# Three weight sums moved from GpSimd to VectorE, and a new written order around the second RMS norm, in a one-core encoder block

## The chip, the cores and the metric

The kernel runs on one core of one Trainium2 chip. The metric is device time in microseconds; the kernel before takes 1011.7 us, the median of three runs (1011.38 to 1012.49). A core has five engines with a queue of instructions each, worked off in order: TensorE (PE in the profile) multiplies matrices into PSUM, VectorE (DVE) does elementwise work, ScalarE (ACT) functions and casts, GpSimd (POOL) elementwise work from SBUF, and SyncE (SP) issues most of the transfers. Semaphores order the engines against each other.

## What is computed

One layer of a hybrid encoder block for 1024 tokens of width 1024, cut here to what matters:

```python
h = rms_norm(x, norm1_g);  q, k, v, u = split(h @ w_in)
a = neighbourhood_attention(rms_norm(q), rms_norm(k), v, rpb)      # 8 heads x 64, window 8 x 16
p = multiscale_pool(u, w_pool, pool_scale)                         # windows 2, 4, 8, 16
x = x + concat(a, p) @ w_out
h2 = rms_norm(x, norm2_g)                                          # x * rsqrt(mean(x*x) + 1e-6) * g
x = x + (silu(h2 @ w_gate) * (h2 @ w_up)) @ w_down                 # D_FF = 2816
```

All of it is in float32.

## The kernel before, in words

**Number format.** TensorE's products are made from split operands. `split(h, l, src)` (L114) casts `src` to a high part `h` on ScalarE (L115) and subtracts it on VectorE for the low part `l` (L116); a product then takes three matmuls, high x high, high x low and low x high. So each operand of each product costs one ScalarE cast and one VectorE subtraction before TensorE can read it.

**Stages.** The projections, the attention and the pooling come first, then the output projection `w_out` (L802), whose tiles `pw` are added into `x2` by VectorE (L818), then the gate and up projections in 22 chunks, and then the down projection. Activations lie transposed, with channels on the partitions. The tokens stand in two halves, `hf` 0 and 1, and the channels in eight blocks, two to an `x2` tile, so `x2[0..3]` is the first token half and `x2[4..7]` the second.

**Gate and up.** A chunk `i` is one pair of column blocks of the gate or the up weights; the chunks alternate between gate and up. A chunk is multiplied as a 2 x 2 block matrix with seven block products in place of eight, in the manner of Strassen and Winograd. `first`, `second`, `part_y`, `part_z`, `part_w`, `part_4` and `part_5` (L1079 to L1132) are these seven, twelve matmuls each. They need sums of weight blocks and of activation blocks:

- `fetch_w(i)` (L1008) loads the raw weights of a chunk in two transfers, issued by SyncE when buffers come free.
- `sum_w(i)` (L1022) makes the three sums s1, s2 and s3, three instructions of 128 x 512 (L1028 to L1030). By default they run on GpSimd; for chunk 3 the call names VectorE.
- `sum_4(i)` (L1018) makes the fourth sum on GpSimd (L1020).
- `cook_w(i, o)` (L1033) splits the weight operand `o`.
- `split_op(o, q, src)` (L999) splits an activation operand, 128 x 1024 per instruction.

**The second norm.** For each half, the squares of `x2` are made on ScalarE (`square`, L948; `square1`, L963), added up (on GpSimd, L950 and `fold`, L956, or on VectorE, L1204), split by `tok_split` (L929) and summed over the partitions by TensorE against a matrix of ones: `tok_sum` (L934), two matmuls, tile `ss`. `scale2(hf)` (L968) makes one over the root: v = mean + eps on VectorE (L973), Ln and Exp on ScalarE (L977, L978), and one correction step of Newton's on VectorE (L979 to L981). `norm2(hf, q)` (L983) multiplies `x2` by the gain and the result (two instructions, L989). For the second half, three `tok_sum` calls stand between `first(0)` and `first(1)` on TensorE's queue, for the tiles `a1`, `s6` and `s7`.

**The order.** From L1154 to L1319 the order on TensorE, ScalarE, VectorE and GpSimd is the order of the text (`pin`, `pin_act`, `pin_dve`, `pin_pool`). Behind that, from chunk 4 on (L1321), the scheduler of the framework puts the instructions of each engine in order, with times of its own. `park` (L1134) makes four sums of the results on GpSimd and stores them. Temporary tiles come from a pool of 45 buffers (`slot`); a load waits until its buffer is free.

Of the kernel before, what the change touches and what calls it, by code (L numbers as in the profile page):

```python
# [9 lines left out]
F32 = mybir.dt.float32  # L10
F32R = mybir.dt.float32r
AF = mybir.ActivationFunctionType
ALU = mybir.AluOpType
# [3 lines left out]
P = 128  # L17
DM = 1024
# [7 lines left out]
EPS = 1e-6  # L26
# [23 lines left out]
def hybrid_block(ctx, tc, xT, xt, w1, wu, rpbx, wpool, wout, wgu, wd, sm, out):  # L50
    nc = tc.nc
# [11 lines left out]
    def slot(dt, name, shape=None):  # L63
        return sp.tile(shape or [P, 1024], dt, tag="t4", name=name)
# [37 lines left out]
    def keep(i):  # L102
        if pin_act:
            tc.keep_in_program_order(i)

    def keepd(i):
        if pin_dve:
            tc.keep_in_program_order(i)

    def keepp(i):  # L110
        if pin_pool:
            tc.keep_in_program_order(i)

    def split(h, l, src):  # L114
        keep(nc.scalar.copy(h, src))  # L115
        keepd(nc.vector.tensor_tensor(out=l, in0=src, in1=h.bitcast(F32), op=ALU.subtract))  # L116
# [32 lines left out]
    def cook_w1_(p, kk):  # L149
        hs = slot(F32R, f"w1h_{p}_{kk}", [P, 2, 384])  # L150
        ls = slot(F32R, f"w1l_{p}_{kk}", [P, 2, 384])
        for i in range(2):
            wp_h[p, 2 * kk + i] = hs[:, i, :]
            wp_l[p, 2 * kk + i] = ls[:, i, :]
        if p == kk == 0:
            raw = raws.pop(("w1", 0, 0))
            keepd(nc.vector.tensor_copy(hs[:, 0], raw[:, 0]))
            yield
            keepd(
                nc.vector.tensor_tensor(out=ls[:, 0], in0=raw[:, 0], in1=hs[:, 0].bitcast(F32), op=ALU.subtract)  # L160
            )
            yield
            split(hs[:, 1], ls[:, 1], raw[:, 1])
        else:
            cook(("w1", p, kk), hs, ls)
# [322 lines left out]
    for i in range(4):  # L488
# [3 lines left out]
        else:  # L492
            g = cook_w1_(0, 0)
# [23 lines left out]
    for t in (6, 7):  # L517
        for k in range(KE, KC):
# [12 lines left out]
            out=qscale, in0=gqk[:, 0:1], scalar=-(HD**-0.5), in1=gqk[:, 1:2], op0=ALU.mult, op1=ALU.mult  # L531
# [270 lines left out]
    def w_out(t, nh, cs, n):  # L802
        ps = bank(stp if n else mmp, f"pw_{t}_{nh}_{n}")
        os_ = slice(t % 4 * P, t % 4 * P + P)
        o, hf = 4 * nh + t % 4, t // 4
        for i, c in enumerate(cs):
            mm3(
                ps,
                wo[c, nh, 0][:, os_],
                wo[c, nh, 1][:, os_],  # L810
                mix[c, hf, 0],
                mix[c, hf, 1],
                i == 0,
                i == len(cs) - 1,
            )
            yield
        x = x2[o // 2 + 4 * hf][:, o % 2]
        keepd(nc.vector.tensor_tensor(out=x, in0=ps, in1=x, op=ALU.add))  # L818
# [8 lines left out]
    x2 = []  # L827
# [89 lines left out]
    op_ = ctx.enter_context(tc.tile_pool(name="op", bufs=1))  # L917
    ones = op_.tile([P, P], F32R, name="ones2")
    nc.gpsimd.memset(ones.bitcast(F32), 1.0)
    ACTO = {}  # L920

    def act_op(o):
        ACTO[o] = [
            [slot(F32R, f"b{o}_{q}_{nm}", [P, 2, 512]) for nm in "hl"] for q in range(2)
        ]

    n2, ps2 = {}, {}

    def tok_split(src, nm):  # L929
        hl = slot(F32R, f"sq_hl_{nm}", [P, 2, 512])  # L930
        split(hl[:, 0], hl[:, 1], src)
        return hl
# [8 lines left out]
    def store(hf, q):  # L941
        keep(nc.scalar.dma_start(out=x2d[q + 4 * hf], in_=x2[q + 4 * hf]))
# [3 lines left out]
    def square(hf, q):  # L946
        s = slot(F32, f"sq_{hf}_{q}", [P, 2, 512])
        keep(nc.scalar.activation(s, x2[q + 4 * hf], AF.Square))  # L948
        if q:
            keepp(nc.gpsimd.tensor_tensor(out=acc[hf], in0=acc[hf], in1=s, op=ALU.add))  # L950
        else:
            acc[hf] = s

    def fold(hf):
        a = acc[hf]
        keepp(nc.gpsimd.tensor_tensor(out=a[:, 0], in0=a[:, 0], in1=a[:, 1], op=ALU.add))  # L956

    def square1(k):
        x = x2[4 + k // 2][:, k % 2]
        if k % 2 == 0:  # L960
            sq1.append(slot(F32, f"sq_1_{k}", [P, 2, 512]))
        r = sq1[-1][:, k % 2]
        keep(nc.scalar.activation(r, x, AF.Square))  # L963
        return r

    sq1 = []

    def scale2(hf):  # L968
        n = slot(F32, f"n2_{hf}", [P, 2, 512])
        n2[hf] = y = slot(F32, f"y2_{hf}", [P, 512])  # L970
        v, a = n[:, 0], n[:, 1]
        keepd(
            nc.vector.tensor_scalar(  # L973
                out=v, in0=ps2[hf], scalar1=1.0 / DM, scalar2=EPS, op0=ALU.mult, op1=ALU.add
            )
        )
        keep(nc.scalar.activation(a, v, AF.Ln))  # L977
        keep(nc.scalar.activation(y, a, AF.Exp, scale=-0.5))  # L978
        keepd(nc.vector.tensor_tensor(out=a, in0=y, in1=y, op=ALU.mult))  # L979
        keepd(nc.vector.scalar_tensor_tensor(out=a, in0=a, scalar=-0.5, in1=v, op0=ALU.mult, op1=ALU.mult))  # L980
        keepd(nc.vector.scalar_tensor_tensor(out=y, in0=a, scalar=1.5, in1=y, op0=ALU.add, op1=ALU.mult))  # L981

    def norm2(hf, *qs):  # L983
        for q in qs:
            x = x2[q + 4 * hf]
            for i in range(2):
                k = 2 * q + i
                keepd(
                    nc.vector.scalar_tensor_tensor(  # L989
                        out=x[:, i],  # L990
                        in0=x[:, i],
                        scalar=g2_sb[:, k : k + 1],
                        in1=n2[hf],
                        op0=ALU.mult,
                        op1=ALU.mult,
                    )
                )

    def split_op(o, q, src):  # L999
        split(*ACTO[o][q], src)  # L1000

# [16 lines left out]
    def sum_4(i):  # L1018
        x = sums[i]["12"]
        keepp(nc.gpsimd.tensor_tensor(out=x, in0=x, in1=sums[i]["s2"], op=ALU.subtract))  # L1020

    def sum_w(i, eng=nc.gpsimd, keep_=keepp):  # L1022
        m, f = MF[i]
        r0, r1 = raww[i]
        sa = slot(F32, f"sa_{m}_{f}", [P, 2, 512])
        s1, s2 = sa[:, 0], sa[:, 1]
        tt = eng.tensor_tensor
        keep_(tt(out=s1, in0=r0[:, 1], in1=r1[:, 1], op=ALU.add))  # L1028
        keep_(tt(out=s2, in0=s1, in1=r0[:, 0], op=ALU.subtract))
        keep_(tt(out=r0[:, 1], in0=r0[:, 0], in1=r0[:, 1], op=ALU.subtract))  # L1030
        sums[i]["s1"], sums[i]["s2"] = s1, s2

    def cook_w(i, o):  # L1033
        if i < EARLY and o in ("11", "12"):
            w = rg.tile([P, 2, 512], F32R, tag="w", name=f"w_{i}_{o}")
        else:
            w = slot(F32R, f"w_{i}_{o}", [P, 2, 512])
        wop[i, o] = w
        if o == "s4" and i > EARLY:
            sum_4(i)  # L1040
        split(w[:, 0], w[:, 1], sums[i][o])

    def product(i, ps, wo_, bo, chain, parts=range(4)):
        w = wop.pop((i, wo_))
        for k in range(4):
            h, l = ACTO[bo][k // 2]
            sl = slice(k * P, k * P + P)
# [102 lines left out]
    def w_full(t, nh, cs=eight, n=2):  # L1150
        for _ in w_out(t, nh, cs, n):
            pass
# [16 lines left out]
    store(1, 0)  # L1169
    fold(0)  # L1170
    hl = tok_split(acc[0][:, 0], "a0")
    for i in range(2):
        for o in ("11", "12"):
            cook_w(i, o)
    for o in ("11", "21"):
        act_op(o)
    w_full(6, 0)
    for i in range(2):
        sum_w(i)
    g = w_out(7, 0, eight, 2)  # L1180
    for _ in range(5):
        next(g)
    tok_sum(0, hl, True, True)
    scale2(0)
    for _ in g:
        pass
    square(1, 1)
    store(1, 1)
    fold(1)
    norm2(0, 0)  # L1190
    split_op("11", 0, x2[0])
    norm2(0, 1)
    fetch_w(2)
    w_full(4, 1)
    r4 = square1(4)
    split_op("11", 1, x2[1])
    sum_w(2)
    norm2(0, 2)
    split_op("21", 0, x2[2])
    w_full(5, 1)  # L1200
    a1 = acc[1][:, 0]
    r5 = square1(5)
    for r in (r4, r5):
        keepd(nc.vector.tensor_tensor(out=a1, in0=a1, in1=r, op=ALU.add))  # L1204
    hl = [tok_split(a1, "a1")]
    norm2(0, 3)
    split_op("21", 1, x2[3])
    store(1, 2)
    for i in range(2):
        sum_4(i)  # L1210
    cook_w(2, "11")
    w_full(6, 1)
    hl.append(tok_split(square1(6), "s6"))
    cook_w(2, "12")
    sum_4(2)
    w_full(7, 1)
    hl.append(tok_split(square1(7), "s7"))
    store(1, 3)
    xs = [bank(stp, f"x_{i}") for i in range(EARLY)]
    first(0, xs[0])  # L1220
    for i in range(3):
        tok_sum(1, hl[i], i == 0, i == 2)
    scale2(1)
    first(1, xs[1])
    fetch_w(3)
# [22 lines left out]
    cook_w(2, "s2")  # L1248
    settle(2, 0, 0, xs[2])
    sum_w(3, nc.vector, keepd)  # L1250
    sum_4(3)
    cook_w(3, "s2")
    act_op("t3")
# [216 lines left out]
    for n in range(len(works)):  # L1470
        g, k = divmod(n, 7)
        last = g == len(DGROUPS) - 1
        o, bo = ORDER[k]
# [99 lines left out]
```

## Time and profile before

| what | value |
|---|---|
| median of three runs | 1011.7 us |
| the profiled execution | 1012.01 us |
| its span in the profile | 1010.0 us |
| TensorE busy | 991.3 us (98%) |
| VectorE busy | 685.1 us (68%) |
| ScalarE busy | 415.7 us (41%) |
| GpSimd busy | 390.6 us (39%) |
| granted TensorE clock, mean | 0.993 |

The profile is one execution. Times in the timeline are microseconds from the start of the span. A row of the timeline reads: start, duration, engine, line, instruction, output tile <- input tiles, shapes, count, and in brackets how long the engine was idle before and which engine and line ended that wait. Neighbouring equal instructions are merged into one row with their count. A row of the waits reads: engine, tile and line <- what it waited for: total us, times, longest. A row of the windows gives, for each engine, the busy time in a stretch, then the granted share of TensorE's clock and the share of the DMA engines that was busy. "PEld" is TensorE's loading of weights, which overlaps its products.

The engines start a VectorE or ScalarE instruction a little before the one ahead has ended, so the distance from start to start is the cost in a full queue, not the duration.

### The profile page before, as it was taken

To read this page: it belongs to the slowest core of one execution; us is meant where nothing else is said; L and a number is where in the kernel's file an instruction comes from. 1 tells how busy PE (TensorE), PEld (TensorE's weight loads), DVE (VectorE), ACT (ScalarE), POOL (GpSimd) and SP (SyncE) were. 2 spreads that over 40 slices of the span, in tenths; PEclk is the share of its full clock that TensorE was granted. 3 is DMA by queue.
4 is the path that set the end of the run, shared out by engine and by line. 5 is a ranking of instruction groups with operands and counts; after the bars stand their busy time and mean duration, and the time that the engine had idled before them with its cause. 6 is when DMAs were issued, how large, how long until landed. Compare 5 with 4: busy or idle time off the path is not lost.

```text
span 1010.0 us, 13253 instructions
## 1 busy us (share of the span) xinstructions
PE 991.3 (98%) x4801; PEld 843.0 (83%) x4801; DVE 685.1 (68%) x1078; ACT 415.7 (41%) x797; POOL 390.6 (39%) x423
## 2 busy tenths in 40 slices
PE   9999999999999959999999999999999999999998
PEld 9988999998888848888888888888888888888887
DVE  5778777657843769877975555555462599888872
ACT  6634666656643234443333233233242254432500
POOL 0001434333422730059867846746733400000170
PEclk9999999999999979999999999999999999999999
DMA  9412742347813220123433322322317983373302
GB/s 352 185 58 88 221 127 73 96 140 249 267 55 139 95 83 1 41 85 115 155 116 116 132 77 104 126 83 105 120 51 243 355 291 127 104 242 113 125 32 94
DMA packets 56177, 135.88 MB, mean 135 GB/s; under 512 B 5872, under 2 KB 14832, under 8 KB 56112
## 3 DMA queue, kind: packets, MB, share of 16 engines
q1 hardware_dynamic: 48032, 106.45, 31.7%
q0 software_dynamic: 6784, 24.38, 6.4%
q10 hardware_dynamic: 1296, 4.21, 1.0%
q8 instruction: 38, 0.62, 0.3%
q14 instruction: 27, 0.22, 0.1%
HBM read 98.05 MB, written 32.77 MB: 130 GB/s over the span
## 4 chain that ended last, share of the span: by engine, by line
PE 85%; DVE 5%; POOL 5%; ACT 2%; issue 2%; DMA 1%; POOLq 0%; ACTq 0%; DVEq 0%
PE pj L85 12%; PE x L85 10%; PE z L85 10%; PE w L85 10%; PE pc L85 6%; PE pa L85 6%; PE pd L85 6%; PE pw L85 5%; PE y L85 5%; PE pu L85 4%; PE pb L85 3%; PE po L85 3%; PE s L85 2%; PE pt L90 2%; POOL gr L1138 1%
## 5 line engine op out<-in xcount | busy, mean ns | idle before, releaser
L85 PE MATMUL x<-b_h,w 128*128 128x512 f32 x352 | 116.3, 394 | 0.0
L85 PE MATMUL pw<-mx,wo 128*128 128x512 f32 x384 | 90.7, 392 | 0.4 <-DVE kl L116 0.4
L85 PE MATMUL pj<-w1h,xh 128*128 128x384 f32 x256 | 87.4, 346 | 1.6 <-DVE vnl L302 1.6
L622 POOL TENSOR_SCALAR e<-e,r 64x128 f32<-64x128 f32 (+2 forms) x96 | 53.8, 576 | 83.0 <-DVE r L617 42.2
L85 PE MATMUL pj<-w1l,xh 128*128 128x384 f32 x256 | 84.8, 335 | 1.0 <-DVE w1l L116 1.0
L85 PEld LDWEIGHTS pw<-mx,wo 128*128 128x128 f32 x384 | 71.0, 188 | 15.4 <-DVE kl L116 0.8
L85 PE MATMUL pj<-w1h,xl 128*128 128x384 f32 x256 | 83.8, 335 | 0.0
L1498 POOL TENSOR_TENSOR x2r<-x2r,u 128x512 f32<-128x512 f32 x12 | 23.8, 2020 | 149.8 <-ACT dbt_h L115 149.8
L1077 POOL TENSOR_TENSOR ur<-ur,gr 128x512 f32<-128x512 f32 x33 | 52.6, 1596 | 74.1 <-DVE ur L1068 31.8
L85 PEld LDWEIGHTS x<-b_h,w 128*128 128x128 f32 x352 | 67.1, 191 | 14.1
L85 PE MATMUL x<-b_l,w 128*128 128x512 f32 x176 | 69.2, 393 | 0.0
L116 DVE TENSOR_TENSOR w_s<-sa,w_s 128x512 fp32r<-128x512 f32 x44 | 52.6, 1196 | 21.9 <-ACT w_s L115 21.7
L115 ACT CAST a_h<-raw_a 128x1024 fp32r<-128x1024 f32 (+1 forms) x42 | 41.0, 978 | 49.3 <-PE pc L85 13.8
L85 PE MATMUL z<-bt_h,w 128*128 128x512 f32 x176 | 57.9, 390 | 0.5 <-DVE gr L1068 0.5
L85 PE MATMUL w<-b_h,w_s 128*128 128x512 f32 x176 | 57.9, 390 | 0.0
L85 PE MATMUL z<-bt_h,w_s 128*128 128x512 f32 x176 | 57.8, 389 | 0.0
L85 PE MATMUL w<-bt_h,w_s 128*128 128x512 f32 x176 | 57.8, 389 | 0.0
L85 PE MATMUL y<-bt_h,w_s 128*128 128x512 f32 x176 | 57.3, 389 | 0.0
L116 DVE TENSOR_TENSOR a_l<-raw_a,a_h 128x1024 fp32r<-128x1024 f32 (+1 forms) x42 | 49.7, 1188 | 3.4 <-ACT a_h L115 3.1
L85 PEld LDWEIGHTS pj<-w1h,xh 128*128 128x128 f32 x256 | 48.5, 190 | 2.8 <-DVE vnl L302 2.3
L85 PEld LDWEIGHTS pj<-w1l,xh 128*128 128x128 f32 x256 | 48.1, 188 | 1.4 <-DVE w1l L116 1.4
L85 PEld LDWEIGHTS pj<-w1h,xl 128*128 128x128 f32 x256 | 48.0, 188 | 0.0
(268 smaller groups left out, 2654.2 us busy)
## 6 DMA issues: line engine op xcount, KB each, us to landing
raw_a<-gsd SPq DMA_DIRECT2D x77, 256.0 KB, 3.7
raw_g<-in_wgu SPq DMA_DIRECT2D x22, 512.0 KB, 4.2
raw_u<-in_wgu SPq DMA_DIRECT2D x22, 512.0 KB, 3.9
gsd<-gr POOLq DMA_DIRECT2D x22, 512.0 KB, 4.0
raw_d<-in_wd SPq DMA_DIRECT2D x20, 512.0 KB, 4.6
nb<-in_rpbx SPq DMA_DIRECT2D x24, 384.0 KB, 4.1
raw_w<-in_w SPq DMA_DIRECT2D x15, 384.0 KB, 4.2
gsd<-ur POOLq DMA_DIRECT2D x11, 512.0 KB, 3.3
```

The costliest lines, as they stand in the source:

```text
L85: i = nc.tensor.matmul(*a, **k)
L90: i = nc.tensor.transpose(*a)
L115: keep(nc.scalar.copy(h, src))
L116: keepd(nc.vector.tensor_tensor(out=l, in0=src, in1=h.bitcast(F32), op=ALU.subtract))
L622: nc.gpsimd.tensor_scalar(out=out, in0=in0, scalar1=s1, scalar2=1.0, op0=ALU.mult, op1=ALU.mult)
L1077: k(eng.tensor_tensor(out=res[i][c][:, l], in0=src, in1=g, op=ALU.mult))
L1138: tt = lambda **k: keepp(nc.gpsimd.tensor_tensor(**k))
L1498: nc.gpsimd.tensor_tensor(out=q, in0=q, in1=U2[c], op=ALU.add)
```

## The change

- `sum_w(0)`, `sum_w(1)` and `sum_w(2)` are issued on VectorE (they were on GpSimd), at other places of the order.
- `scale2`: Ln reads the sum in PSUM itself, with scale 1/1024 and a bias tile `eps`; the square of the Exp result is made on ScalarE and no longer by L979 on VectorE; `scale2` takes a list of functions that it issues between the square and the rest of the correction step. v is still made on VectorE.
- For the first half that list holds `seven`: the rest of output tile `(7, 0)`, its square, store and fold, `sum_w(1)` and `sum_4(1)`. `sum_4(0)` is put ahead of `scale2(0)`.
- The splits of the first operands (`"11"`, `"21"`), the `norm2` calls and the splits for the token sums are put in another order, in which a `norm2` or another VectorE instruction stands between a cast and its low part.
- `fetch_w(2)` and `w_full(4, 1)` stand one `norm2` earlier; `cook_w(1, ...)` stands behind `w_full(6, 0)`; `sum_4(2)` stands behind `sum_w(3)`.

```diff
+    eps = op_.tile([P, 1], F32, name="eps")
+    nc.gpsimd.memset(eps, EPS)
...
-    def scale2(hf):
+    def scale2(hf, between=()):
...
-        keep(nc.scalar.activation(a, v, AF.Ln))
+        keep(nc.scalar.activation(a, ps2[hf], AF.Ln, scale=1.0 / DM, bias=eps))
         keep(nc.scalar.activation(y, a, AF.Exp, scale=-0.5))
-        keepd(nc.vector.tensor_tensor(out=a, in0=y, in1=y, op=ALU.mult))
+        keep(nc.scalar.activation(a, y, AF.Square))
+        for f in between:
+            f()
         keepd(nc.vector.scalar_tensor_tensor(out=a, in0=a, scalar=-0.5, in1=v, op0=ALU.mult, op1=ALU.mult))
...
     hl = tok_split(acc[0][:, 0], "a0")
-    for i in range(2):
-        for o in ("11", "12"):
-            cook_w(i, o)
     for o in ("11", "21"):
         act_op(o)
+    cook_w(0, "11")
+    cook_w(0, "12")
     w_full(6, 0)
-    for i in range(2):
-        sum_w(i)
+    cook_w(1, "11")
+    cook_w(1, "12")
+    sum_w(0, nc.vector, keepd)
     g = w_out(7, 0, eight, 2)
     for _ in range(5):
         next(g)
     tok_sum(0, hl, True, True)
-    scale2(0)
-    for _ in g:
-        pass
-    square(1, 1)
-    store(1, 1)
-    fold(1)
+
+    def seven():
+        for _ in g:
+            pass
+        square(1, 1)
+        store(1, 1)
+        fold(1)
+        sum_w(1, nc.vector, keepd)
+        sum_4(1)
+
+    sum_4(0)
+    scale2(0, (seven,))
     norm2(0, 0)
-    split_op("11", 0, x2[0])
-    norm2(0, 1)
     fetch_w(2)
     w_full(4, 1)
     r4 = square1(4)
+    norm2(0, 1)
+    split_op("11", 0, x2[0])
+    norm2(0, 2)
     split_op("11", 1, x2[1])
-    sum_w(2)
-    norm2(0, 2)
-    split_op("21", 0, x2[2])
     w_full(5, 1)
     a1 = acc[1][:, 0]
     r5 = square1(5)
+    norm2(0, 3)
     for r in (r4, r5):
         keepd(nc.vector.tensor_tensor(out=a1, in0=a1, in1=r, op=ALU.add))
+    split_op("21", 0, x2[2])
     hl = [tok_split(a1, "a1")]
-    norm2(0, 3)
     split_op("21", 1, x2[3])
     store(1, 2)
-    for i in range(2):
-        sum_4(i)
+    w_full(6, 1)
+    r6 = square1(6)
+    sum_w(2, nc.vector, keepd)
+    hl.append(tok_split(r6, "s6"))
+    w_full(7, 1)
+    r7 = square1(7)
     cook_w(2, "11")
-    w_full(6, 1)
-    hl.append(tok_split(square1(6), "s6"))
+    hl.append(tok_split(r7, "s7"))
     cook_w(2, "12")
-    sum_4(2)
-    w_full(7, 1)
-    hl.append(tok_split(square1(7), "s7"))
     store(1, 3)
...
     sum_w(3, nc.vector, keepd)
+    sum_4(2)
     sum_4(3)
```

## The prediction

> **What bounds the kernel now.** I read the page first, then TensorE's waits, then the stretch that holds them in windows and engine by engine in the timeline. The page gives the span; the profiled run itself took 1012.01 us, 2.0 us more than its span, and lies 0.3 us above the median of 1011.7.
>
> ```profile
> span 1010.0 us, 13253 instructions
> ```
>
> TensorE's waits (total, times, longest):
>
> ```profile
> PE ss L85 <- ACT sq_hl_s L115: 7.5, 2, 5.8
> PE ss L85 <- ACT sq_hl_a L115: 2.6, 1, 2.6
> ...
> PE z L85 <- DVE gr L1068: 0.5, 1, 0.5
> ```
>
> So TensorE, which is busy nearly everywhere else, loses some 10 us at one place: the six small products `ss` that sum the squares of the second token half. They are queued behind `first(0)`, and everything else of TensorE stands behind them. The windows show that the stretch loses time a second way (columns: PE, PEld, DVE, ACT, POOL busy, granted clock, DMA share, GB/s):
>
> ```profile
> 350.00:400.00 50.00, 39.63 (x156) 30.86 (x155) 39.46 (x48) 19.25 (x29) 11.31 (x8) 0.86 0.12 43
> ...
> 367.00:368.00 1.00, 0.04 (x1) 0.00 (x0) 0.81 (x2) 0.10 (x1) 0.00 (x0) 1.00 0.58 234
> 368.00:369.00 1.00, 0.00 (x0) 0.00 (x0) 0.02 (x1) 1.00 (x2) 0.00 (x0) 0.53 0.27 106
> ...
> 381.00:382.00 1.00, 1.00 (x5) 0.77 (x4) 0.93 (x3) 0.00 (x0) 0.00 (x0) 0.64 0.00 0
> ```
>
> TensorE is idle 10.4 of these 50 us, and the clock stands at half from 368.1 to about 381.7, into the dense products again. TensorE's timeline:
>
> ```profile
> 336.50 23.96 PE L85 MATMUL pw<-mx,wo 128*128 128x512 f32 x105
> ...
> 365.82 0.50 PE L85 MATMUL ss<-sq_hl_a,ones 128*128 128x512 f32 x1 [2.64 <-ACT sq_hl_a L115]
> ...
> 372.83 1.52 PE L85 MATMUL ss<-sq_hl_s,ones 128*128 128x512 f32 x2 [5.79 <-ACT sq_hl_s L115]
> 376.07 1.52 PE L85 MATMUL ss<-sq_hl_s,ones 128*128 128x512 f32 x2 [1.72 <-ACT sq_hl_s L115]
> 377.39 0.63 PE L85 MATMUL x<-b_h,w 128*128 128x512 f32 x1
> ...
> 398.47 0.39 PE L85 MATMUL y<-bt_h,w_s 128*128 128x512 f32 x1
> ```
>
> 105 products in 23.96 us are 0.228 us each, so one product of twelve takes 2.73 us. The last output tile is done at 360.5, `first(0)` at 363.2, and then TensorE waits. From 377.39 to the first `y`, 84 products (seven times twelve) take 21.1 us, where 84 x 0.228 is 19.1: 2.0 us go to the half clock.
>
> What the `ss` products wait for is VectorE's queue. Its add of the last output tile, which ScalarE's square waits for, comes 13.5 us after TensorE finished that tile:
>
> ```profile
> 333.47 3.48 DVE L116 TENSOR_TENSOR w<-raw_g,w 128x512 fp32r<-128x512 f32 x2
> ...
> 340.27 0.68 DVE L818 TENSOR_TENSOR x<-pw,x 128x512 f32<-128x512 f32 x1
> ...
> 344.42 0.69 DVE L981 SCALAR_TENSOR_TENSOR y<-n,y 128x512 f32<-128x512 f32 x1
> ...
> 348.20 2.18 DVE L116 TENSOR_TENSOR b_l<-x,b_h 128x1024 fp32r<-128x1024 f32 x1 [1.18 <-ACT b_h L115]
> 350.31 3.48 DVE L989 SCALAR_TENSOR_TENSOR x<-x,sm_sb,y 128x512 f32<-128x512 f32 x2
> ...
> 366.41 1.41 DVE L989 SCALAR_TENSOR_TENSOR x<-x,sm_sb,y 128x512 f32<-128x512 f32 x2
> 368.98 1.23 DVE L116 TENSOR_TENSOR b_l<-x,b_h 128x1024 fp32r<-128x1024 f32 x1 [1.17 <-ACT b_h L115]
> 370.12 0.68 DVE L116 TENSOR_TENSOR w<-raw_g,w 128x512 fp32r<-128x512 f32 x1
> 370.72 0.68 DVE L818 TENSOR_TENSOR x<-pw,x 128x512 f32<-128x512 f32 x1
> ...
> 374.02 0.69 DVE L818 TENSOR_TENSOR x<-pw,x 128x512 f32<-128x512 f32 x1
> ```
>
> ```profile
> 330.46 1.29 POOL L956 TENSOR_TENSOR sq<-sq 128x512 f32<-128x512 f32 x1
> ...
> 339.76 1.74 POOL L1030 TENSOR_TENSOR raw_u<-raw_u 128x512 f32<-128x512 f32 x1
> 346.88 2.42 POOL L950 TENSOR_TENSOR sq<-sq,sq 128x1024 f32<-128x1024 f32 x1 [5.38 <-ACT sq L948]
> ...
> 374.25 1.26 POOL L1020 TENSOR_TENSOR raw_g<-raw_g,sa 128x512 f32<-128x512 f32 x1 [14.13 <-DVE w L116]
> ```
>
> The same VectorE instruction costs 0.60 us (start to start, 370.12 to 370.72) with GpSimd idle and 1.74 beside a GpSimd sum; that sum stretches from about 1.28 to 1.74. They take turns. An add from PSUM stays at 0.68 at 340.27, while GpSimd is in its sum of 339.76: only VectorE instructions with both inputs in SBUF are held. The Trainium skill, page "SBUF — State Buffer", section "Who interferes with whom", says that the loser is blocked for the whole instruction; the trace agrees (`b_l` of 348.20 runs 2.18, to just over one 1.1 us after the 346.88 sum ends). One GpSimd sum therefore costs a busy VectorE about 1.1 us.
>
> **The change part by part.**
>
> ```profile
> 342.30 0.63 ACT L978 ACTIVATE y<-n 128x512 f32<-128x512 f32 x1
> 345.74 1.06 ACT L948 ACTIVATE sq<-x 128x1024 f32<-128x1024 f32 x1 [2.81 <-DVE x L818]
> ```
>
> ```profile
> 377.63 0.69 DVE L973 TENSOR_SCALAR n<-ss 128x512 f32<-128x512 f32 x1 [0.89 <-PE ss L85]
> ...
> 396.10 1.23 DVE L116 TENSOR_TENSOR bt_l<-t,bt_h 128x1024 fp32r<-128x1024 f32 x1 [0.52 <-ACT bt_h L115]
> ...
> 398.45 0.68 DVE L1028 TENSOR_TENSOR sa<-raw_u,raw_u 128x512 f32<-128x512 f32 x1
> 399.16 0.69 DVE L1029 TENSOR_TENSOR sa<-sa,raw_u 128x512 f32<-128x512 f32 x1
> 399.77 0.69 DVE L1030 TENSOR_TENSOR raw_u<-raw_u 128x512 f32<-128x512 f32 x1
> ```
>
> *Sums on VectorE.* Chunk 3's sum is already there: 0.71 + 0.61 + 0.69, 2.0 us. Three more are 6.0 us of VectorE. Nine GpSimd sums go, worth 9 x 1.1 = 9.9 us if VectorE was held by each.
>
> *Root.* In `scale2` L973 leaves the chain (`Ln` reads PSUM with scale and bias itself), and L979 becomes a Square on ScalarE of 0.63 us. One 0.69 us instruction and its hop leave the chain: 0.7 to 0.8 us for each half. Square stands behind Exp with nothing loaded between (342.30, 345.74), so no table load is added.
>
> *The new order*, on the clock of the old trace. ScalarE's four casts are done by 334.5:
>
> ```profile
> 332.43 1.11 DVE L116 TENSOR_TENSOR sq_hl_a<-sq,sq_hl_a 128x512 fp32r<-128x512 f32 x1 [4.34 <-ACT sq_hl_a L115]
> ...
> 333.35 1.14 ACT L115 CAST w<-raw_u 128x512 fp32r<-128x512 f32 x2
> ```
>
> From 332.43 VectorE's `sq_hl` low, four `w` lows and one add then take 0.60 each instead of up to 1.74, so `sum_w(0)` runs from 336.0 to 338.0, before v. The add of `(7, 0)` waits for its product (336.50 + 9 x 0.228, about 338.8); queued behind it are `sum_w(1)` and the end of the root. Its square (1.06) releases GpSimd's L950 at 340.6. From there GpSimd has 2.42 + 1.29 + 1.26 = 5.0 us (`square`, `fold`, `sum_4(1)`), and takes turns with the last instruction of `sum_w(1)` and the two of the root: y is done at 340.7 + 5.0 + 3 x 0.6, 347.5. Before it was 345.1. So the first root comes 2.4 us **later**.
>
> After that GpSimd is out of the way until the last low parts. VectorE's list up to the add of the last tile: three adds 1.8, eight `norm2` 4.8, four `b_l` at 1.14 to 1.23 4.6, two additions into a1 1.3, its low and that of s6 1.2, `sum_w(2)` 2.0: 15.7 us, and 0.6 of waiting for the cast behind r4, the one low part whose cast isn't a step ahead. Add(7,1) then starts at 347.5 + 16.3 = 363.8, against 374.02: 10.2 us earlier. The last `ss` began 2.8 us after it (376.07 opens a pair of 1.52, so the second comes some 0.75 later); now chunk 2's cast stands between square and cast, some 0.4 us. So `first(1)` starts at 363.8 + 2.8 + 0.4 + 0.5 = 367.5, 9.9 us earlier. TensorE's remaining idle time is about 3 us, most of it one gap of 2.0 between s6 and s7.
>
> *What is late next.* `y` needs the low part of the second `t2`, ready at 397.33, 19.7 us after v; now that is 367.6 + 19.7 - 0.8, 386.5. TensorE would be at `y` at 367.5 + 19.1 = 386.6, and reads this low part 1.6 us in: covered by 1.7 us. If that cover goes, each us late costs one.
>
> *Answers of nothing.* `eps` is one memset far ahead. `act_op` only names buffers. The loads of chunk 2 hold their place: SyncE issues them when buffers come free. Chunk 3's second load waited for L1204, which comes 7 us earlier:
>
> ```profile
> 357.77 7.64 SPq L1013 DMA_DIRECT2D raw_u<-in_wgu  x2
> ```
>
> `store(1,1)` on ScalarE's queue follows a square as it did. `sum_4(2)` stands later in the text, but GpSimd's queue holds nothing between.
>
> *Clock.* Whether the 2.0 us come back rests on the gap. In the old trace the clock fell at 368.1, 4.9 us after the dense products ended, though no idle time until then was above 2.64 us; in those 4.9 us TensorE had two products of 0.50, 1.0 us of work. The new stretch, 363.2 to 367.5, is 4.3 us long and holds all six `ss`, 6 x 0.23 to 6 x 0.50, 1.4 to 3 us of work; but from 364.3 to 367.1 there is one product only. Bounds: 0, or the 2.0 us again, perhaps 3. I take 0: the new stretch ends sooner and holds more work than the one after which the clock fell.
>
> The Trainium skill, page "TensorE: Matmul & The Clock Gate", section "Part 1: The HAM clock gate", has the clock fall after an idle window of about 3.4 us, free-running. By that the clock should have stood until 370.5, 3.4 us after the work of 367.04, and the trace has 368.1; by the page alone the new kernel keeps the full clock and the sum stands.
>
> *Sum.* 9.9 + 2.0 = 11.9 us: 1012.0 - 11.9 = 1000.1 for such a profiled run, 999.8 against the median.
>
> **The rivals.**
>
> 1. *The clock falls all the same.* For it: the fall of 368.1 on a window that was not empty. Against: the shorter gap. The products lose 2 to 3 us again: 1001.8 to 1002.8.
>
> 2. *VectorE stays behind.* GpSimd's 5.0 us fall just where the root is made, and the add of `(7, 0)` is a wait ahead of it. If it also holds ScalarE's order up, so that all four `b_l` wait for their casts as in the old trace (1.18 at 348.20, 1.17 at 368.98), that is 4 x 1.2 less the 0.6 counted, 4.2 us; the gap is then long enough for the half clock, 2.0 more. 5.7 us of the gain are left: 1006, and 1008 if GpSimd holds VectorE two turns longer.
>
> 3. *The free order behind turns against it (slower).* From chunk 4 on the order isn't written out; the scheduler picks it from estimated times, and an edit ahead can give another. GpSimd has almost no slack where that part begins:
>
> ```profile
> 440.00:480.00 40.00, 40.00 (x178) 33.14 (x177) 31.25 (x30) 14.33 (x27) 38.33 (x29) 1.00 0.29 99
> ```
>
> The old order lost 0.5 us there (`z`). A `sum_w` or `park` set one product too early in each of the 18 chunks from 4 on would make TensorE wait; from 0.7 us a chunk (12 us) the gain is gone, and 0.85 us gives 1015. Against: the old trace has no such wait after 505.
>
> 4. *Nothing changes*, because the gap only moves to `y`: that needs `t2` 10 us later than worked out; nothing shows it. 1010 to 1012.
>
> **How the numbers follow.** Forecast 0.54; rival 1 0.25; rival 2 0.11; rival 3 0.06; rival 4 0.04. No change is within 0.2%, 2 us, which a measurement of this kernel can tell. Forecast, rivals 1 and 2 are faster: 0.90; same 0.04; slower 0.06. The forecast's own range is 997.0 (TensorE's remaining 3 us vanish as well) to 1001.5; with rival 1 and the nearer part of rival 2 the range is 997 to 1006.
>
> **What would show it.** In the new profile: GpSimd without L1028 to L1030 before 400; `w` lows at 0.6 to 0.7 us; y of the first half about 347.5, later than before; the add of the last tile about 364; PE's waits at `ss` about 3 us in all; granted clock 1.00 from 350 to 400; `y` at about 386.6 without a wait; PE's wait at about 493 still below 1 us. I am wrong if the add of the last tile comes after 368, if the clock falls, or if a wait at `y` or beyond chunk 4 takes the gain.

## The result, and the profile after

The changed kernel takes 1001.04 us (median of four runs, 1000.26 to 1001.68), the kernel before beside it 1011.93 us. The ratio is 0.9892, with a 95% interval of 0.9875 to 0.9909: 10.9 us less, where 11.9 were forecast. The profiled run took 1001.02 us.

TensorE's waits in the profile of the changed kernel (total, times, longest); 10 us at `ss` have become 2.0, and one wait at `z` is new:

```profile
span 999.2 us, 13246 instructions
...
PE ss L85 <- ACT sq_hl_s L115: 1.7, 1, 1.7
...
PE z L85 <- DVE gr L1072: 0.5, 1, 0.5
PE z L85 <- DVE w_s L116: 0.5, 1, 0.5
...
PE ss L85 <- DVE sq_hl_s L116: 0.3, 1, 0.3
```

The window from 350 to 400 (busy PE, PEld, DVE, ACT, POOL, then granted clock, DMA share, GB/s): TensorE is busy 48.0 us of 50 where it was 39.6, GpSimd 2.8 where it was 11.3, and the clock is full.

```profile
350.00:400.00 50.00, 47.99 (x211) 39.19 (x210) 45.48 (x59) 26.37 (x39) 2.81 (x2) 1.00 0.12 43
```

TensorE's timeline. The row of 337.20 answers to that of 336.50 before, so this execution was 0.7 us later when the changed stretch began. That belongs to the execution and not to the kernel: profiled once more, the changed kernel has this row at 336.51, and in the other profiled runs, of kernels old and new, it starts anywhere from 336.25 to 337.43. Where times of two runs are compared below as counted from this row, that difference is taken out.

```profile
337.20 23.96 PE L85 MATMUL pw<-mx,wo 128*128 128x512 f32 x105
...
366.50 0.49 PE L85 MATMUL ss<-sq_hl_s,ones 128*128 128x512 f32 x1 [1.70 <-ACT sq_hl_s L115]
367.31 0.50 PE L85 MATMUL ss<-sq_hl_s,ones 128*128 128x512 f32 x1 [0.31 <-DVE sq_hl_s L116]
367.65 0.39 PE L85 MATMUL x<-b_h,w 128*128 128x512 f32 x1
...
386.71 0.39 PE L85 MATMUL y<-bt_h,w_s 128*128 128x512 f32 x1
...
403.03 0.39 PE L85 MATMUL z<-bt_h,w_s 128*128 128x512 f32 x1
403.26 0.39 PE L85 MATMUL z<-bt_l,w_s 128*128 128x512 f32 x1
404.10 0.74 PE L85 MATMUL z<-bt_h,w_s 128*128 128x512 f32 x2 [0.46 <-DVE w_s L116]
...
406.54 0.39 PE L85 MATMUL w<-bt_h,w_s 128*128 128x512 f32 x1
```

`first(1)` starts at 367.65 (before: 377.39) and the first `y` at 386.71 (before: 398.47), 11.8 us earlier. At the end of the critical chain, the `z` that waits for GpSimd's work, the gain is smaller. That wait ended at 505.43 before:

```profile
494.71 3.02 PE z L85 x12
```

So 10.7 us are left there, and the span is 10.8 us shorter. One us was lost between `y` and this `z`.

VectorE's timeline, in the part that answers to the rows of before: the `w` lows run in 0.60 each, the last add stands at 364.08 (before: 374.02), and only one low part among the first operands still waits for its cast, 0.32 us.

```profile
333.75 1.29 DVE L116 TENSOR_TENSOR w<-raw_g,w 128x512 fp32r<-128x512 f32 x2
...
342.70 2.77 DVE L985 SCALAR_TENSOR_TENSOR y<-n,y 128x512 f32<-128x512 f32 x1
345.50 3.36 DVE L993 SCALAR_TENSOR_TENSOR x<-x,sm_sb,y 128x512 f32<-128x512 f32 x2
...
349.38 1.40 DVE L993 SCALAR_TENSOR_TENSOR x<-x,sm_sb,y 128x512 f32<-128x512 f32 x2
351.10 1.23 DVE L116 TENSOR_TENSOR b_l<-x,b_h 128x1024 fp32r<-128x1024 f32 x1 [0.32 <-ACT b_h L115]
...
364.08 0.68 DVE L818 TENSOR_TENSOR x<-pw,x 128x512 f32<-128x512 f32 x1
...
367.85 0.69 DVE L975 TENSOR_SCALAR n<-ss 128x512 f32<-128x512 f32 x1
...
371.35 0.69 DVE L985 SCALAR_TENSOR_TENSOR y<-n,y 128x512 f32<-128x512 f32 x1
```

GpSimd in the same stretch: three instructions, which stand exactly beside the stretched ones of VectorE (2.77 for 0.69, 3.36 for 1.41).

```profile
342.51 2.41 POOL L952 TENSOR_TENSOR sq<-sq,sq 128x1024 f32<-128x1024 f32 x1 [2.59 <-ACT sq L950]
345.00 1.62 POOL L958 TENSOR_TENSOR sq<-sq 128x512 f32<-128x512 f32 x1
346.58 1.73 POOL L1024 TENSOR_TENSOR raw_u<-raw_u,sa 128x512 f32<-128x512 f32 x1
```

ScalarE, the two `Ln`: each still waits for v.

```profile
339.46 0.69 ACT L979 ACTIVATE n<-ss,eps 128x512 f32<-128x512 f32 x1 [4.27 <-DVE n L975]
...
368.57 0.69 ACT L979 ACTIVATE n<-ss,eps 128x512 f32<-128x512 f32 x1 [1.12 <-DVE n L975]
```

The order of TensorE's and SyncE's instructions is the same in both kernels, and the scheduler's order from chunk 4 on is the same on all engines, so rival 3 did not come up.

### The profile page after: what moved, and what is told of

It is laid out like the page before. It is cut to its first block, busy times and chain, and to the rows that moved or that the text cites. A ratio compares the mean times of both kernels' runs of the same rounds, so it can differ in the third digit from the quotient of the medians.

```text
span 999.2 us, 13246 instructions
## 1 busy us (share of the span) xinstructions
PE 987.4 (99%) x4801; PEld 840.1 (84%) x4801; DVE 686.4 (69%) x1085; ACT 415.9 (42%) x799; POOL 374.4 (37%) x415
## 4 chain that ended last, share of the span: by engine, by line
PE 81%; DVE 8%; POOL 5%; ACT 2%; issue 2%; DMA 1%; SPq 0%; POOLq 0%; DVEq 0%
PE pj L85 11%; PE w L85 10%; PE z L85 10%; PE x L85 8%; PE pw L85 6%; PE pc L85 6%; PE pa L85 6%; PE pd L85 6%; PE y L85 4%; PE pu L85 4%; PE pb L85 3%; PE po L85 3%; PE s L85 2%; PE pt L90 1%; POOL gr L1142 1%
```

## The experiments

All times are medians; "before" is the old kernel run beside them on the same chip, and the ratio is to it.

| kernel | us | before | ratio (95%) |
|---|---|---|---|
| sums alone | 1010.69 | 1012.21 | 0.9986 (0.9976 to 0.9995) |
| order and root, sums on GpSimd | 1005.96 | 1012.21 | 0.9942 (0.9926 to 0.9959) |
| new, old root | 1001.73 | 1012.21 | 0.9901 (0.9886 to 0.9916) |
| new, third sum in the root | 1001.83 | 1012.21 | 0.9898 (0.9884 to 0.9913) |
| new, once more | 1000.91 | 1012.49 | 0.9885 (0.9868 to 0.9901) |
| new, late fourth sum | 999.78 | 1012.49 | 0.9878 (0.9863 to 0.9892) |
| that, and squares added on VectorE | 998.87 | 1012.49 | 0.9868 (0.9853 to 0.9882) |
| old, gap filled with products | 1011.41 | 1012.49 | 0.9988 (0.9978 to 0.9997) |
| new, lows at once | 1008.07 | 1012.70 | 0.9954 (0.9939 to 0.9968) |
| new, Ln first | 1000.90 | 1012.70 | 0.9881 (0.9865 to 0.9898) |
| squares on VectorE, and Ln first | 998.89 | 1012.70 | 0.9866 (0.9851 to 0.9881) |

**The sums alone.** The old kernel, with

```diff
     for i in range(2):
-        sum_w(i)
+        sum_w(i, nc.vector, keepd)
...
-    sum_w(2)
+    sum_w(2, nc.vector, keepd)
```

> The old kernel with its three weight sums on VectorE at their old places; order and root are the old ones. Three theories of where the 10.9 us come from. A, the order: in the old order each low part of an operand waits for its cast right ahead of it (1.2 us, four times), GpSimd's fourth sums move up into the stretch in which the first norm is applied, and VectorE gets 6.0 us more to do; worked through row by row the low part of the second half's first square sum comes at about 365.7, against 365.8 in the old kernel: 1010.5 to 1012 us, the clock falls as before. B, the sums: the change is worth what GpSimd's turns cost, nine times 1.1 us: 1001 to 1004, TensorE's waits at the square sums under 4 us. C, both halves alike: about 1006.

It takes 1.5 us off: 1010.69, inside the range that theory A gave; B and C are out. VectorE's timeline shows why. The `w` lows and the sums run in 0.60 to 0.72, but each low part stands right behind its cast and waits for it, and GpSimd's fourth sums have moved up beside the first norm (the last two rows):

```profile
347.01 2.17 DVE L116 TENSOR_TENSOR b_l<-x,b_h 128x1024 fp32r<-128x1024 f32 x1 [1.17 <-ACT b_h L115]
349.10 3.47 DVE L989 SCALAR_TENSOR_TENSOR x<-x,sm_sb,y 128x512 f32<-128x512 f32 x2
...
354.81 1.23 DVE L116 TENSOR_TENSOR b_l<-x,b_h 128x1024 fp32r<-128x1024 f32 x1 [1.64 <-ACT b_h L115]
...
360.46 1.23 DVE L116 TENSOR_TENSOR b_l<-x,b_h 128x1024 fp32r<-128x1024 f32 x1 [1.18 <-ACT b_h L115]
```

```profile
350.28 1.73 POOL L1020 TENSOR_TENSOR raw_g<-raw_g,sa 128x512 f32<-128x512 f32 x1
351.98 1.73 POOL L1020 TENSOR_TENSOR raw_u<-raw_u,sa 128x512 f32<-128x512 f32 x1
```

The low part that theory A put at 365.7 came 1.3 us earlier, at 364.42.

**Order and root without the sums.** The new kernel, with

```diff
-    sum_w(0, nc.vector, keepd)
+    sum_w(0)
...
-        sum_w(1, nc.vector, keepd)
+        sum_w(1)
...
-    sum_w(2, nc.vector, keepd)
+    sum_w(2)
```

> The new kernel with its three weight sums back on GpSimd, at the places of the new order. A, the order: GpSimd's nine sums cost VectorE about 1.1 us each, but 6.0 us of its own work go, and some of the turns fall on additions from PSUM, which aren't held; the add of the last tile comes 1 to 4 us later than 364.1: 1002 to 1006, the upper end if the clock falls. B, the sums: 1009 to 1012, TensorE's waits near the old 10 us. C: about 1006.

6.3 us of the gain stay, 1005.96, at the top of what A allowed (C had named the same number, but C fails at the sums alone). So the two parts are worth 6.3 and 1.5 us alone, 7.8 together, and 10.9 to 11.6 when both are made: some 3 to 4 us need both. With the sums on GpSimd they fall beside the first norm. VectorE's norm of 2 x 0.6 us takes 4.46, the next 2.87:

```profile
344.09 4.46 DVE L993 SCALAR_TENSOR_TENSOR x<-x,sm_sb,y 128x512 f32<-128x512 f32 x2
348.48 0.68 DVE L818 TENSOR_TENSOR x<-pw,x 128x512 f32<-128x512 f32 x1
349.08 2.87 DVE L993 SCALAR_TENSOR_TENSOR x<-x,sm_sb,y 128x512 f32<-128x512 f32 x2
...
366.88 0.68 DVE L818 TENSOR_TENSOR x<-pw,x 128x512 f32<-128x512 f32 x1
```

The last add is 2.8 us later than in the new kernel, 3.2 counted from the row of the 105 products, and the clock falls (mean 0.93 from 350 to 400). Part of it is a lost cover: without `sum_w(2)` ahead of it the low part of s6 waits 1.41 us for its cast (365.95).

**The low parts at once.** The new kernel with the norms and splits back where they stood:

```diff
     norm2(0, 0)
+    split_op("11", 0, x2[0])
+    norm2(0, 1)
     fetch_w(2)
     w_full(4, 1)
     r4 = square1(4)
-    norm2(0, 1)
-    split_op("11", 0, x2[0])
-    norm2(0, 2)
     split_op("11", 1, x2[1])
+    norm2(0, 2)
+    split_op("21", 0, x2[2])
     w_full(5, 1)
...
     r5 = square1(5)
-    norm2(0, 3)
...
-    split_op("21", 0, x2[2])
     hl = [tok_split(a1, "a1")]
+    norm2(0, 3)
     split_op("21", 1, x2[3])
```

> The new kernel with one part of its order undone: the norms and the four splits of the first operands stand as in the old kernel, so that each low part follows its cast at once. If the cast waits are what the new order removes, VectorE waits about 1.2 us at each of the four, the cast of the square sum 0.7 more; less what GpSimd's turns hid at the first, add(7,1) comes 3.5 to 5 us later, the clock falls for two windows instead of one: 1005 to 1008 beside 1001. Rival, the waits are hidden by GpSimd's turns or by what follows: 1001 to 1002.

It costs about 7 us, 1008.07, just past the upper edge of what was expected; the rival is out. The five waits can be read off VectorE's timeline, 5.9 us in all, against 0.32 in the new kernel, and the last add is 5.5 us later, 5.9 counted from the row of the 105 products:

```profile
349.60 1.23 DVE L116 TENSOR_TENSOR b_l<-x,b_h 128x1024 fp32r<-128x1024 f32 x1 [1.18 <-ACT b_h L115]
...
354.39 1.23 DVE L116 TENSOR_TENSOR b_l<-x,b_h 128x1024 fp32r<-128x1024 f32 x1 [1.64 <-ACT b_h L115]
...
358.12 1.23 DVE L116 TENSOR_TENSOR b_l<-x,b_h 128x1024 fp32r<-128x1024 f32 x1 [1.18 <-ACT b_h L115]
...
362.08 0.69 DVE L116 TENSOR_TENSOR sq_hl_a<-sq,sq_hl_a 128x512 fp32r<-128x512 f32 x1 [0.74 <-ACT sq_hl_a L115]
...
365.27 1.23 DVE L116 TENSOR_TENSOR b_l<-x,b_h 128x1024 fp32r<-128x1024 f32 x1 [1.17 <-ACT b_h L115]
...
369.54 0.69 DVE L818 TENSOR_TENSOR x<-pw,x 128x512 f32<-128x512 f32 x1
```

**The old root.** The new kernel, with

```diff
-        keep(nc.scalar.activation(a, ps2[hf], AF.Ln, scale=1.0 / DM, bias=eps))
+        keep(nc.scalar.activation(a, v, AF.Ln))
         keep(nc.scalar.activation(y, a, AF.Exp, scale=-0.5))
-        keep(nc.scalar.activation(a, y, AF.Square))
         for f in between:
             f()
+        keepd(nc.vector.tensor_tensor(out=a, in0=y, in1=y, op=ALU.mult))
```

> The new kernel with the old root: Ln reads v, the square of the Exp result is VectorE's. A: each root is 0.7 us longer; the first puts the add of the last tile 0.7 us later, the second takes 0.7 of the 0.8 us by which the second low part of t2 comes ahead of its use: 0.7 to 1.4 us more, 1001.7 to 1002.5. Rival, the root lies off the path: 1001.0, unchanged. Rival, the root carries a large part: 1004 or more.

1001.73, where the new kernel has 1001.04 and 1000.91: as expected in size, but the differences lie inside the intervals, and the reason was half wrong. The second root takes as long with either: from the start of v to the end of y 4.20 us in this run (368.32 to 372.52), 4.19 in the new kernel (367.85 to 372.04), and 4.19 before (377.63 to 381.82). What the new root saves is one VectorE instruction in the full queue of the first half, not a link of the chain: counted from the row of the 105 products, the last add comes 0.9 us later with the old root (364.55 - 336.81 = 27.74 against 364.08 - 337.20 = 26.88), and so does `y`.

**Ln first.** The new kernel with `Ln` issued ahead of v:

```diff
+        keep(nc.scalar.activation(a, ps2[hf], AF.Ln, scale=1.0 / DM, bias=eps))
         keepd(
             nc.vector.tensor_scalar(
...
-        keep(nc.scalar.activation(a, ps2[hf], AF.Ln, scale=1.0 / DM, bias=eps))
```

> The new kernel with two lines exchanged: in the root Ln is issued ahead of v. In the new kernel's trace Ln waits for v at both halves (4.3 and 1.1 us idle before it), though it reads the sum itself: the framework orders two readers of one PSUM tile. With Ln ahead, v waits for Ln, and nothing waits for v. The second root then is done 0.7 us earlier; TensorE's loss at z of about 1 us, which VectorE behind the root sets, shrinks by as much: 0.5 to 0.9 us less, 1000.0 to 1000.5 beside 1001. Rival, GpSimd's chain alone sets the time of z: no change.

Now v waits for `Ln`, so the two are put in order as they stand in the text. What orders them stays open: both read the same PSUM tile, and both write a half of the same tile `n`; no run separates the two.

```profile
368.11 0.69 ACT L974 ACTIVATE n<-ss,eps 128x512 f32<-128x512 f32 x1 [0.40 <-PE ss L85]
```

```profile
368.83 0.69 DVE L976 TENSOR_SCALAR n<-ss 128x512 f32<-128x512 f32 x1 [0.72 <-ACT n L974]
```

`Ln` starts 0.4 us after the last `ss`. The second root is shorter, as expected: from the end of the last `ss` to the end of its last VectorE instruction 3.56 us (368.07 to 371.63), where the new kernel has 4.23 (367.81 to 372.04). But the time does not move, 1000.90: a miss. The clock fell in the profiled run (0.97 from 350 to 400), `y` came at 388.60 and there was no wait at `z` for VectorE that could shrink. The last kernel below has the same edit with a full clock.

**The third sum in the root.** The new kernel, with

```diff
-    sum_w(2, nc.vector, keepd)
     hl.append(tok_split(r6, "s6"))
...
-    scale2(1)
+    scale2(1, (partial(sum_w, 2, nc.vector, keepd),))
```

> The new kernel with the third weight sum (2.0 us on VectorE) taken out from ahead of the last add and put where VectorE waits for ScalarE's root of the second half (2.1 us idle). If TensorE's remaining gap of 1.7 us is set by VectorE's queue up to that add, the add comes 1.9 us earlier, the gap closes to under 0.5 us and everything behind moves by 1.5 to 2: 999.0 to 999.6. Rival: VectorE behind the root is the bound, the cover at y or z is used up, and nothing comes through: 1001.0.

A miss, 1001.83. The sum had been the cover of a cast: without it VectorE waits 1.41 us for the cast of s6, so the add comes only 0.5 us earlier (363.59). The sum isn't free in the root either: VectorE's first instruction behind it (370.34) runs 1.54 us beside a GpSimd sum, and the second root takes 5.04 us (367.57 to 372.61) in place of 4.19. And in this run the clock fell after a shorter gap than the new kernel has:

```profile
366.02 0.49 PE L85 MATMUL ss<-sq_hl_s,ones 128*128 128x512 f32 x1 [1.29 <-ACT sq_hl_s L115]
366.83 0.70 PE L85 MATMUL ss<-sq_hl_s,ones 128*128 128x512 f32 x1 [0.31 <-DVE sq_hl_s L116]
```

```profile
366.00:367.00 1.00, 0.67 (x2) 0.36 (x3) 1.00 (x3) 0.97 (x2) 0.00 (x0) 0.98 1.00 410
367.00:368.00 1.00, 1.00 (x3) 0.81 (x4) 0.81 (x2) 0.00 (x0) 0.00 (x0) 0.50 0.07 25
370.00:371.00 1.00, 1.00 (x5) 0.81 (x4) 0.85 (x2) 0.31 (x1) 1.00 (x1) 0.82 0.00 0
```

It is at half from about 366.96 to 370.36, 3.4 us. The fall doesn't explain the miss: the one run of the four with a mean clock of 1.00 was the slowest, 1002.14.

**The gap of the old kernel filled.** The old kernel with products that nobody reads:

```diff
+    wps_ = bank(mmp, "gap_fill")
     for i in range(3):
         tok_sum(1, hl[i], i == 0, i == 2)
+        for n in range((22, 5, 0)[i]):
+            mm(wps_, ones, hl[0][:, n % 2], start=True, stop=True)
```

> The old kernel with 27 products added that nobody reads, 22 in TensorE's gap ahead of the second pair of square sums and 5 ahead of the third, 0.23 us each; they fit into the waits of 5.8 and 1.7 us. What the half clock costs by itself: if the 2.0 us of the sum are right, the clock stays at 1.00 from 350 to 400 and the time is 1009.7 to 1010.3 beside 1012. If the half clock cost nothing, since VectorE behind it set the end: 1012.

1.1 us less, between the two. The clock still fell, at 368.5 during the first fill products, but was full again at 371.9, before the real ones. From the last `ss` to `y` are 19.4 us, as in the new kernel at the full clock (367.31 to 386.71):

```profile
377.48 0.50 PE L85 MATMUL ss<-sq_hl_s,ones 128*128 128x512 f32 x1 [0.23 <-DVE sq_hl_s L116]
...
396.88 0.39 PE L85 MATMUL y<-bt_h,w_s 128*128 128x512 f32 x1
```

So the products got their 2.0 us, and a wait of 0.5 at `z` for `w_s` appeared, the same as in the new kernel. Of the 2.0 us, 1.1 reach the end; the interval, 0.3 to 2.2 us, doesn't exclude all of it.

**The new kernel once more, and two steps on.** The late fourth sum:

```diff
         sum_w(1, nc.vector, keepd)
-        sum_4(1)
...
     sum_4(2)
+    sum_4(1)
     sum_4(3)
```

The second step adds to it

```diff
-        square(1, 1)
+        s11.append(slot(F32, "sq_1_1", [P, 2, 512]))
+        keep(nc.scalar.activation(s11[0], x2[5], AF.Square))
         store(1, 1)
-        fold(1)
...
     norm2(0, 3)
+    keepd(nc.vector.tensor_tensor(out=acc[1], in0=acc[1], in1=s11[0], op=ALU.add))
+    keepd(nc.vector.tensor_tensor(out=a1, in0=a1, in1=acc[1][:, 1], op=ALU.add))
```

> The new kernel once more, as the measure for the two kernels run beside it: 1000.5 to 1001.8 us.

> The new kernel with one GpSimd instruction moved: the fourth sum of chunk 1, which in the new kernel runs at 346.6 and takes turns with VectorE's first norm, stands behind that of chunk 2 and so runs at about 369, where VectorE waits for ScalarE's root. If GpSimd's instructions between 342 and 348 hold VectorE on the path to the last add, that add comes 1.0 to 1.2 us earlier and the time falls by 0.5 to 1.1: 1000.0 to 1000.6 beside 1001.1. Rival, the bound lies behind the root (z waits 0.5 for VectorE already): no change, 1001.1.

> As the kernel with the late fourth sum, and the two additions of squares that GpSimd makes inside the first root are VectorE's too, behind the norm (1.14 + 0.71 us). GpSimd then does nothing from 340 to 367. It held VectorE for 4.0 us there (2.77 less 0.69, and 3.36 less 1.41), so the last add comes 4.0 - 1.85 = 2.2 us earlier, TensorE's gap of 1.7 us at the square sums closes, and the clock cannot fall: 998.8 to 999.6 beside 1001.1. Rival, VectorE behind the root is the bound: 1000.5 to 1001.1.

1000.91 and 998.87 lie in their ranges, 999.78 is 0.2 us below its own. The steps are in the traces too: counted from the row of the 105 products, the last add comes 1.0 us earlier with the late fourth sum and 1.9 us with the squares on VectorE. No run of the second step (998.5 to 999.28) reaches the times of the eight runs of the new kernel (999.85 to 1001.68), so the rival is out; the first step alone has one run (1000.4) among them. In the second step GpSimd does nothing between 340 and 365, VectorE's end of the root and first norm are no longer stretched, and TensorE waits 0.3 us in all at `ss`:

```profile
342.47 0.69 DVE L985 SCALAR_TENSOR_TENSOR y<-n,y 128x512 f32<-128x512 f32 x1
343.20 1.41 DVE L993 SCALAR_TENSOR_TENSOR x<-x,sm_sb,y 128x512 f32<-128x512 f32 x2
...
361.90 0.69 DVE L818 TENSOR_TENSOR x<-pw,x 128x512 f32<-128x512 f32 x1
```

All four runs of it show a mean clock of 1.00. Taking GpSimd's work away from VectorE's queue is thus worth about 2 us inside the new kernel, after VectorE's own work for the squares (1.85 us) and with what the falling clock costs there.

**Both.** That kernel, and `Ln` first.

> The kernel with the squares' additions on VectorE and the late fourth sum, and Ln ahead of v. The two act on different waits, the gap at the square sums and the loss at z: 998.0 to 998.5, 0.4 to 0.9 under the 998.9 of the first alone. Rival: 998.9, unchanged.

998.89, no change: a miss again in time, though in the profiled runs the wait at `z` for `w_s` goes from 0.4 to 0.2 us and the span from 997.2 to 996.7. Half a microsecond is less than these times can tell apart.

So the best kernel here is the one with no GpSimd work beside VectorE's queue, 998.87 us, 2 us under the changed kernel.

## Why the prediction was right, step by step

**The path.** Right. The add of the last tile was put at 363.8 and came at 364.08, in an execution that was 0.7 us late. `first(1)` was put at 367.5 and came at 367.65. TensorE waited 2.0 us at `ss` where about 3 were forecast.

**How much each part carries.** The prediction costed the sums at 6.0 us added against 9.9 removed, and the new order as one list. The runs split it: the order carries most of what one part gives alone (6.3 us, and undoing the four splits costs 7), the sums little alone (1.5). The reason is that removing the turns leaves the cast waits in place, 5.9 us in each of the three kernels that have the low parts at once, and removing the cast waits lets GpSimd's sums fall on the norms. A queue that is late for two reasons is freed by removing both.

**The first root.** Wrong. It was to be 2.4 us later than before, at 347.5; it was done at 342.70 + 2.77 = 345.5, or 344.8 without the 0.7 of the late start. The step that failed is "its square (1.06) releases GpSimd's L950 at 340.6": ScalarE made that square only behind Ln, Exp and Square, which waited for v, so GpSimd came at 342.5 and held the end of the root and the norm, 2.1 + 1.9 = 4.0 us. Even so the end came out nearly the same: by the forecast the first norm ends at 347.5 + 1.2 = 348.7, and it did at 348.78, or 348.1 without the late start. GpSimd came 1.2 us later than forecast, but less of VectorE's work was left to take turns with it; that the two nearly cancelled was luck. The list behind held.

**"L973 leaves the chain."** Wrong. Ln reads the PSUM tile, but it was put in order behind v, which stood first (1.12 us of waiting, the row of 368.57). The chain kept its 4.19 us. The 0.7 to 0.8 us for each half were not there. The cover at `y` was 0.8 us in place of 1.7 (the second low part of t2 was done at 386.31 + 1.23, 0.8 us before its use 1.6 us into `y`), which was still enough, since `y` didn't wait.

**The clock.** The price of 2.0 us in the products is right (filling the gap gave them back), but the fall isn't decided by the length of the gap alone. The new kernel, profiled once more, shows the same gap as in the first profile (1.72 us, there 1.70), and this time the clock fell:

```profile
365.82 0.50 PE L85 MATMUL ss<-sq_hl_s,ones 128*128 128x512 f32 x1 [1.72 <-ACT sq_hl_s L115]
```

```profile
350.00:400.00 50.00, 47.98 (x204) 39.01 (x203) 45.35 (x58) 25.80 (x38) 2.80 (x2) 0.97 0.12 43
```

Of the eight timed runs of the new kernel four have a mean clock of 0.998, as this one, and four 0.999 or 1.00, as the first profile. So rival 1 was not another way for the kernel to go but a draw in each execution, and the full clock of the first profile was partly luck. The fall costs about 0.7 us (means of 1001.2 and 1000.5; four runs each, which spread by as much), less than forecast. The two profiles agree: counted from the row of the 105 products, `y` comes 1.6 us later with the fallen clock, and the end of the span 0.6 us later. The next point explains the difference.

**What is late next.** Here a loss was put at nothing: 11.9 us were forecast, 10.9 measured. `y` was covered and came 11.8 us earlier, 12.5 counted from the row of the 105 products, which is 0.6 more than forecast. But the prediction stopped there. From `y` on TensorE ran ahead of VectorE by the 2.0 us that the full clock returned: the low parts of the t1 operand were done 12.4 us after `y` before (408.50 + 2.35 against 398.47) and 14.3 after. The second `z` needs a low part that stands in VectorE's queue behind these, and lost 0.46 us by waiting and 0.79 in all (3.51 us from its start at 403.03 to the next product at 406.54, where others take 2.72). A later `w`, from 422.87 to 425.84, took 2.97 and lost 0.25 more, its weights waiting for a `w_s` of VectorE. Together they are the one us lost between `y` and the late `z`; 11.4 of the 12.5 us are left. In the profile with the fallen clock neither loss occurs; the two take each other's place, which leaves the 0.6 us of above. That shortening this loss would shorten the kernel was argued from the traces; `Ln` first, which should have reduced it, showed nothing in the times.

**The free order.** It did not change, and the wait of 0.5 us for GpSimd is at 494.7, where 493 was forecast; the chain from the last `w` ahead of GpSimd's work to this `z` takes 63.3 us in both kernels (442.17 to 505.43 before, 431.45 to 494.71 after), so it moved with TensorE.

## What to carry to other kernels

When one engine's queue is late, list everything that holds it, turns with another engine and waits for a cast right ahead alike, and expect less than the sum from removing only one. An instruction that seems to be in the way can be the cover of another wait, as the third sum was for a cast. Work out what is late next for every consumer behind the stall, not only the first, since TensorE freed from a stall and from a half clock runs ahead of the engines that feed it.

## What the runs showed of the hardware

The clock can fall after gaps much shorter than the 3.4 us that it then stays down: 1.72 and 0.31 us of idle time with small products between were enough in one execution of the new kernel, 1.70 and 0.31 were not in another, and 1.29 and 0.31 were enough with the third sum in the root. In the 3.4 us ahead of its fall TensorE was busy for 1.0 us in the old kernel (364.65 to 368.06), 1.4 in the new one (363.43 to 366.84), 1.6 with `Ln` first (365.23 to 368.64) and 1.8 with the third sum in the root (363.56 to 366.97). The Trainium skill, page "TensorE: Matmul & The Clock Gate", section "Part 1: The HAM clock gate", has the clock fall after an idle window of about 3.4 us, free-running. The half clock of 366.96 to 370.36 agrees with that length, but the 3.4 us ahead of it were not idle: by these runs a partly filled window is enough.

An ACTIVATE of 128 x 512 took 0.69 us in the new `Ln`, which has a bias tile and reads PSUM, and 0.63 in the old `Ln` and in `Exp`, which have no bias tile and read SBUF; no run separates the two.
